# Local attention: two triangular probability blocks added, transposed and split as one, then separated by two GpSimd selections

## The chip, the core and the metric

The kernel runs on one core of a Trainium2 chip. A core has a matrix engine (TensorE, PE in the profile), three engines for element-wise work (VectorE or DVE, ScalarE or ACT, GpSimd or POOL), a queue that issues transfers (SyncE or SP), a scratch memory of 128 partitions (SBUF) and an accumulator memory (PSUM). Each engine works through its own instructions in order; semaphores make one engine wait for another. The metric is the device time of one execution in microseconds.

## The reference, cut to what matters

A decoder block with two parallel mixers over 1024 tokens, and a feed-forward part behind them. The change concerns the first mixer, local attention with a window of 128 keys: eight query heads in two groups of four, each group with one key/value head of width 64.

```
qb = q.reshape(B, nb, BLOCK, SWA_KV_HEADS, SWA_GROUP, HEAD_DIM)       # 8 blocks of 128 queries
...
diff = qi - kj + BLOCK                     # kj over 256 keys: the block before, and its own
band_ok = (diff >= 0) & (diff < WINDOW)
...
s = jnp.where(mask[None, :, None, None], s, -jnp.inf)
...
p = jnp.exp(s - m)
denom = jnp.sum(p, axis=-1, keepdims=True) + jnp.exp(sink - m)
p = (p / denom).astype(v.dtype)
o = jnp.einsum('bnhgqk,bnkhd->bnqhgd', p, vw)
```

For query `q` of a block, the allowed keys of the block before are those with index `k > q`, and those of its own block are `k <= q`. The probability block 128 x 256 of a head is therefore an upper and a lower triangle that complement each other, and all else in it is zero. The first block has no block before it.

## The kernel before, in words

All matrix products are made at nearly full float32 accuracy out of rounded parts: an operand is split into a high part (rounded copy, by ACT) and a low part (source minus high part, by DVE); the helper is `split` (L161 to L166). `mm3` (L168 to L174) issues three matmuls for a product: high by high, high by low, low by high.

Local attention runs in sixteen iterations, `it` = 0 to 15: group `it // 8`, query block `it % 8`. Iterations 0 and 8 are first blocks and have one key block, all others two. The iterations are threaded with `gate_step()` (L843), which issues one step of another, larger product (the gate projections): twelve matmuls of 128x512 with their weights split three steps ahead by ACT and DVE, and sums of weight tiles ("mixes", L177 and L180, 128x256 pieces) on POOL. The loop is L1018 to L1035. In iteration `it` it issues, in this order: a load of queries (`sw_q`), a gate step, the query transposes of `it+1` (`sw_qT`), a gate step, the value product of `it-1` (`sw_pv`), the scores and softmax of `it+1` (`sw_scores`), a gate step, and the probability transposes of `it` (`sw_pT`).

- `sw_scores` (L898 to L933): eight matmuls give the scores of four heads. DVE adds the band mask and takes the maximum (L914), ACT takes the exponentials with their sums (L926), and POOL adds the sink's term (L928), inverts the denominators (L929) and multiplies the probabilities `pe` (128 x 4 x 256) by them, a head at a time (L931).
- `sw_pT` (L935 to L944): for each key block, TensorE transposes the four heads' 128x128 blocks into one PSUM tile (L943), and `split` writes its high and low parts to `pth` and `ptl`.
- `sw_pv` (L946 to L965): for each key block two matmuls (L954 on `pth`, L955 on `ptl`) with the values as weights, then a copy on ACT (L957) and two additions on DVE (L962, L963).

TensorE and SP take their instructions in the order in which the program writes them (`in_order`, L328). In this loop ACT, DVE and POOL are ordered by a planner at build time, by its own costs; on the chip each of them is then in order too.

Of the kernel before, what the change touches and what calls it, by code (L numbers as in the profile page):

```python
# [9 lines left out]
F32R = mybir.dt.float32r  # L10
BF16 = mybir.dt.bfloat16
AF = mybir.ActivationFunctionType
ALU = mybir.AluOpType
# [4 lines left out]
P = 128  # L18
# [71 lines left out]
def hybrid_block_kernel(  # L90
# [29 lines left out]
    nc = tc.nc  # L120
# [19 lines left out]
    def uid(name):  # L140
        counter[0] += 1
        return f"{name}_{counter[0]}"

    def U(name, dt=F32, shape=(P, 1024)):
        return pool.tile(list(shape), dt, tag="u", name=uid(name))
# [4 lines left out]
    def tiny(name, w=1):  # L150
        return small.tile([P, w], F32, tag=f"t{w}", name=uid(name))

    def P1(name, shape=(P, 512)):
        return ps1.tile(list(shape), F32, tag="ps", name=uid(name))

    def PX(name, shape=(P, 512)):
        return psum["x"].tile(list(shape), F32, tag="ps", name=uid(name))
# [3 lines left out]
    def split(hi, lo, src, eng=None):  # L161

        i = nc.scalar.copy(hi, src)  # L163
        if held[0]:
            tc.keep_in_program_order(i)
        (eng or nc.vector).tensor_tensor(lo, src, hi.bitcast(F32), op=ALU.subtract)  # L166
# [15 lines left out]
    def blk(b, n=1):  # L182
        return slice(b * P, (b + n) * P)
# [5 lines left out]
    ident = const.tile([P, P], F32, name="ident")  # L189
# [708 lines left out]
    def sw_scores(it):  # L898
        g, b = divmod(it, NB)
        d = sw[it]  # L900
        qs = d.pop("qs")
        c0 = P if b == 0 else 0
        kc = slice((b - 1) * P + c0, (b + 1) * P)
        mx = tiny("mx", 4)
        scs = []
        for hp in range(2):
            sc = PX("sc", (P, 2, 2 * P))
            scs.append(sc)
            for j in range(2):
                nc.tensor.matmul(sc[:, j, c0:], qs[:, hp, j], khd[g][0][:, kc], start=True, stop=False)  # L910
                nc.tensor.matmul(sc[:, j, c0:], qs[:, hp, j], khd[g][1][:, kc], start=False, stop=True)
            for j in range(2):
                h = 2 * hp + j
                nc.vector.tensor_tensor_reduce(sc[:, j, c0:], sc[:, j, c0:], band[:, c0:], 1.0, NEG, op0=ALU.add,  # L914
                                               op1=ALU.max, accum_out=mx[:, h:h + 1])
        ns = nsink[:, 4 * g:4 * g + 4]
        nm = tiny("nm", 4)
        nc.vector.scalar_tensor_tensor(nm, mx, -SC_A, ns, op0=ALU.mult, op1=ALU.min)
        es = tiny("es", 4)
        nc.vector.tensor_tensor(es, nm, ns, op=ALU.subtract)  # L920
        den = tiny("den", 4)
        pe = U("pe", F32, (P, 4, 2 * P))
        for h in range(4):
            if h == 1:
                nc.scalar.activation(es, es, AF.Exp)
            nc.scalar.activation(pe[:, h, c0:], scs[h // 2][:, h % 2, c0:], AF.Exp, scale=SC_A, bias=nm[:, h:h + 1],  # L926
                                 accum_out=den[:, h:h + 1])
        nc.gpsimd.tensor_tensor(den, den, es, op=ALU.add)  # L928
        nc.gpsimd.tensor_tensor(den, den, neg_one, op=ALU.pow)  # L929
        for h in range(4):  # L930
            nc.gpsimd.tensor_scalar(pe[:, h, c0:], pe[:, h, c0:], den[:, h:h + 1], 0.0, op0=ALU.mult, op1=ALU.add)  # L931
        d["pe"] = pe
        d["kbs"] = [1] if b == 0 else [0, 1]  # L933

    def sw_pT(it):  # L935
        d = sw[it]
        pe = d.pop("pe")
        d["pth"] = U("pth", F32R, (P, 2, 4, P))
        d["ptl"] = U("ptl", F32R, (P, 2, 4, P))
        for kb in d["kbs"]:  # L940
            pp = P1("pT", (P, 4, P))
            for h in range(4):
                nc.tensor.transpose(pp[:, h], pe[:, h, blk(kb)], ident)  # L943
            split(d["pth"][:, kb], d["ptl"][:, kb], pp)  # L944

    def sw_pv(it):  # L946
        g, b = divmod(it, NB)
        d = sw.pop(it)
        kbs = d["kbs"]
        po = P1("o", (P, 2, 2, P))  # L950
        for kb in kbs:
            kblk = b - 1 + kb
            vst = vv[kblk // 4][:, kblk % 4, g]
            nc.tensor.matmul(po, vst, d["pth"][:, kb], start=kb == kbs[0], stop=False)  # L954
            nc.tensor.matmul(po, vst, d["ptl"][:, kb], start=False, stop=kb == 1)  # L955
        tmp = U("ot", F32, (P, 2, 2, P))
        nc.scalar.copy(tmp[0:64], po[64:128])  # L957
        if b % 4 == 0:
            oa_t[it // 4] = U("oa", F32, (P, 2, 512))
        oa = oa_t[it // 4]  # L960
        oc = blk(b % 4)
        nc.vector.tensor_tensor(oa[0:64, :, oc], po[0:64, :, 0], tmp[0:64, :, 0], op=ALU.add)  # L962
        nc.vector.tensor_tensor(oa[64:128, :, oc], po[0:64, :, 1], tmp[0:64, :, 1], op=ALU.add)  # L963
        if b % 4 == 3:
            nc.sync.dma_start(oa_d[it // 4], oa_t.pop(it // 4))  # L965
# [6 lines left out]
    for i, b in enumerate((4, 5, 6, 7, 0, 1, 2, 3)):  # L972
        ps = P1("kl", (P, KVL))
        mm3(ps, [(hT(k, blk(b)), (wkl[k // 4][0][:, k % 4], wkl[k // 4][1][:, k % 4])) for k in range(NK)])
        t = U("lat", F32, (P, 2, KVL))
        nc.scalar.copy(t[:, 0], ps)
        ss = tiny("ss")
        nc.scalar.activation(t[:, 1], t[:, 0], AF.Square, accum_out=ss)
        r = rstd_of(ss, KVL)
        if i == 0:  # L980
            latent_end(NB - 1)
            sw_qT(0)
            while lat_out:
                lat_store()
        if i == 2:
            gates.prep_to(1)
        if i == 3:
            gates.mix(0, nc.vector)
        if i == 4:
            sw_scores(0)  # L990
            gates.prep_to(2)
        if i >= 4:
            t4_of_h(i - 4)
        scaled.append((t, r, b))
        if i == 4:
            gates.load_part(1, 0)
        while len(scaled) > (2 if i < 5 else 1):
            kv_out(*scaled.pop(0))
# [19 lines left out]
    for it in range(N_SW):  # L1018
        if it + 2 < N_SW:
            sw_q(it + 2)  # L1020
        gate_step()
        if it + 1 < N_SW:
            sw_qT(it + 1)
        gate_step()
        if it >= 1:
            sw_pv(it - 1)
        if it + 1 < N_SW:
            sw_scores(it + 1)
        if it == N_SW - 1:
            load_lat(4)  # L1030
        gate_step()
        sw_pT(it)
    gate_step()
    gate_step()
    sw_pv(N_SW - 1)  # L1035
    in_order.__exit__(None, None, None)

# [233 lines left out]
    for t in range(NT):  # L1271
        h, n = divmod(t, NB)
# [509 lines left out]
```

## Time and profile before

| | |
|---|---|
| median of 3 runs | 1357.79 us (1356.15 to 1358.18) |
| span of the profiled execution | 1357.9 us |
| PE busy | 1338.8 us, 99% |
| DVE busy | 914.3 us, 67% |
| ACT busy | 641.1 us, 47% |
| POOL busy | 557.1 us, 41% |

The profile gives no other time for its execution than the span. Engines run beside each other, so busy shares add up to more than one. The local-attention loop lies between about 151 and 329 us.

In a row of the timeline stand the start and the length in us, the engine, the line, the operation, what it writes and reads, its shape and its count; in brackets, how long the engine had stood idle and what ended that. In a row of groups stand the count, the sum in us and the mean in ns, then the idle time before them.

### The profile page before, as it was taken

The page shows a single profiled execution, that of the slowest core. Times are in us where ns is not written, and L with a number is a line of the kernel's source. Part 1 is how long each engine was busy: PE and PEld are TensorE (multiplying, and loading weights), DVE is VectorE, ACT ScalarE, POOL GpSimd, SP SyncE. Part 2 cuts the span into 40 slices and gives each one's busy share as a digit, 9 for nine tenths or more (in the row PEclk, how much of TensorE's full clock was granted, in tenths as well). Part 3 has the DMA queues.
Part 4 walks back from the last instruction along what each step waited for, and adds up shares of the span by engine and source line. Part 5 has one row for each costly group of instructions (what it writes and reads, how often), then busy time and mean ns, then how long its engine had stood idle before and what let it go on. Part 6 is the DMA issues. An engine that isn't in the chain of part 4 may idle for free.

```text
span 1357.9 us, 18990 instructions
## 1 busy us (share of the span) xinstructions
PE 1338.8 (99%) x6600; PEld 1122.6 (83%) x6600; DVE 914.3 (67%) x1495; ACT 641.1 (47%) x1299; POOL 557.1 (41%) x610
## 2 busy tenths in 40 slices
PE   9999999999999999999999999999999999999997
PEld 6899878878888888888887888888888888888886
DVE  6868767776777787585448866666656654664862
ACT  7433767665567777651336232322332332644443
POOL 1115545553166554200031465766665551022521
PEclk9999999999999999999999999999999999999999
DMA  9454322335100110671243353644434425996504
GB/s 359 162 182 157 115 102 83 101 129 179 54 1 13 44 47 17 250 239 55 112 167 134 127 175 143 228 178 178 151 137 178 164 85 180 380 380 245 171 11 145
DMA packets 78239, 202.25 MB, mean 149 GB/s; under 512 B 8768, under 2 KB 15424, under 8 KB 78144
## 3 DMA queue, kind: packets, MB, share of 16 engines
q1 hardware_dynamic: 76704, 198.68, 41.2%
q10 hardware_dynamic: 1440, 2.36, 0.5%
q8 instruction: 52, 0.85, 0.2%
q14 instruction: 43, 0.35, 0.1%
HBM read 141.24 MB, written 59.77 MB: 148 GB/s over the span
## 4 chain that ended last, share of the span: by engine, by line
PE 79%; DVE 8%; ACT 4%; issue 3%; POOL 3%; DMA 2%; SPq 0%; POOLq 0%; ACTq 0%; DVEq 0%
PE fa L174 7%; PE fa L172 7%; PE fa L173 7%; PE fb L174 6%; PE fb L173 6%; PE fb L172 6%; PE fd L172 5%; PE fd L174 5%; PE fd L173 5%; PE xo L172 2%; PE xo L174 2%; PE xo L173 2%; PE pTb L1170 1%; PE oA L172 1%; PE oA L174 1%
## 5 line engine op out<-in xcount | busy, mean ns | idle before, releaser
L166 DVE TENSOR_TENSOR wl<-wr,wl 128x512 fp32r<-128x512 f32 x150 | 153.6, 1048 | 72.3 <-ACT wl L163 71.9
L166 DVE TENSOR_TENSOR lrv<-lr,lrv 128x1024 fp32r<-128x1024 f32 x77 | 104.9, 1396 | 48.6 <-ACT lrv L163 44.5
L163 ACT CAST lrv<-lr 128x1024 fp32r<-128x1024 f32 x77 | 80.1, 1052 | 94.1 <-PE fd L174 55.6
L172 PE MATMUL fd<-lrv 128*128 128x512 f32 x308 | 119.8, 389 | 0.0
L173 PE MATMUL fd<-lrv 128*128 128x512 f32 x308 | 119.8, 389 | 0.0
L174 PE MATMUL fd<-lrv 128*128 128x512 f32 x308 | 119.8, 389 | 0.0
L177 POOL TENSOR_TENSOR wr<-wr,sm 128x512 f32<-128x512 f32 (+1 forms) x38 | 46.4, 1229 | 150.8 <-DVE wl L166 117.2
L163 ACT CAST wl<-wr 128x512 fp32r<-128x512 f32 x150 | 86.9, 623 | 2.1 <-DVE wr L828 1.9
L304 POOL TENSOR_SCALAR ms<-ss 128x1 f32<-128x1 f32 x32 | 8.7, 271 | 189.8 <-ACT xn L1546 111.5
L166 DVE TENSOR_TENSOR wl<-sm,wl 128x512 fp32r<-128x512 f32 x60 | 47.2, 812 | 46.0 <-ACT wl L163 45.9
L174 PEld LDWEIGHTS fd<-lrv 128*128 128x128 f32 x308 | 57.8, 188 | 12.1
L173 PEld LDWEIGHTS fd<-lrv 128*128 128x128 f32 x308 | 57.8, 188 | 12.1
L172 PEld LDWEIGHTS fd<-lrv 128*128 128x128 f32 x308 | 57.8, 188 | 11.8
L1155 POOL TENSOR_TENSOR denb<-denb,neg_one 128x1 f32<-128x1 f32 x64 | 38.0, 594 | 69.2 <-ACT p L1154 56.8
L1154 ACT ACTIVATE p<-scb,nmb 128x384 f32<-128x384 f32 (+3 forms) x64 | 47.6, 744 | 38.4 <-DVE nmb L1153 36.5
L166 DVE TENSOR_TENSOR ptl<-pTb,pth 128x512 fp32r<-128x512 f32 (+2 forms) x96 | 50.5, 550 | 14.0 <-ACT pth L163 13.4
L1153 DVE CUSTOM_DVE_ANT_0 scb<-scb,mask 128x384 f32<-128x384 f32 (+3 forms) x64 | 48.5, 758 | 13.1 <-PE scb L1145 12.5
L1438 ACT ACTIVATE act<-sm 128x512 f32<-128x512 f32 x11 | 7.0, 633 | 104.9 <-DVE sm L180 104.9
L1156 POOL TENSOR_SCALAR p<-p,denb 128x384 f32<-128x384 f32 (+3 forms) x64 | 49.4, 773 | 6.3
L163 ACT CAST pth<-pTb 128x512 fp32r<-128x512 f32 (+2 forms) x96 | 43.3, 482 | 12.2 <-PE pTb L1170 11.6
L172 PE MATMUL fb<-t2h,wl 128*128 128x512 f32 x120 | 47.4, 395 | 0.0
L172 PE MATMUL fb<-t3h,wl 128*128 128x512 f32 x120 | 47.3, 394 | 0.0
(348 smaller groups left out, 4310.2 us busy)
## 6 DMA issues: line engine op xcount, KB each, us to landing
lr<-la_d SPq DMA_DIRECT2D x77, 256.0 KB, 5.4
wr<-in_w_gate_dram SPq DMA_DIRECT2D x22, 512.0 KB, 3.9
wr<-in_w_up_dram SPq DMA_DIRECT2D x22, 512.0 KB, 5.1
wd<-in_w_down_dram SPq DMA_DIRECT2D x22, 512.0 KB, 6.6
rb_d<-wd SPq DMA_DIRECT2D x22, 512.0 KB, 2.6
la_d<-sd SPq DMA_DIRECT2D x22, 512.0 KB, 5.3
lr<-rb_d SPq DMA_DIRECT2D x44, 256.0 KB, 5.4
lr<-in_w_down_dram SPq DMA_DIRECT2D x33, 256.0 KB, 5.8
```

The lines of the kernel that those rows point to most:

```text
L163: i = nc.scalar.copy(hi, src)
L166: (eng or nc.vector).tensor_tensor(lo, src, hi.bitcast(F32), op=ALU.subtract)
L172: nc.tensor.matmul(ps, ah, bh, start=first and i == 0, stop=False, skip_group_check=go_on)
L173: nc.tensor.matmul(ps, ah, bl, start=False, stop=False, skip_group_check=go_on)
L174: nc.tensor.matmul(ps, al, bh, start=False, stop=last and i == n - 1, skip_group_check=go_on)
L177: eng.tensor_tensor(out, a, b, op=ALU.subtract)
L304: nc.gpsimd.tensor_scalar(ms, ss, 1.0 / width, EPS, op0=ALU.mult, op1=ALU.add)
L1153: nc.vector.tensor_tensor_reduce(s_, s_, m_, 1.0, -NEG, op0=ALU.add, op1=ALU.min, accum_out=nm)
L1154: nc.scalar.activation(p_, s_, AF.Exp, scale=-1.0, bias=nm, accum_out=den)
L1155: nc.gpsimd.tensor_tensor(den, den, neg_one[:, 0:1], op=ALU.pow)
L1156: nc.gpsimd.tensor_scalar(p[:, 0:w], p[:, 0:w], den, 0.0, op0=ALU.mult, op1=ALU.add)
L1170: nc.tensor.transpose(pp[:, i], p[:, blk(k0 + i)], ident)
```

## The change

For every iteration with two key blocks, POOL now adds the two halves of `pe` before the multiplication, which then covers 128 columns a head and not 256. `sw_pT` transposes four blocks and not eight, and splits once, into one tile `x` that holds the high and the low part (128 x 2 x 4 x 128). Two affine selections on POOL then separate the triangles: one writes a second tile `y` with the entries `q >= k` of the own block and zeros elsewhere, the other clears these in `x`, in place, so that `x` keeps the block before. `sw_pv` issues the same four matmuls on slices of `x` and `y`. First blocks (iterations 0 and 8) have one half, one transposition of four blocks and no selection.

```diff
+        if b:
+            nc.gpsimd.tensor_tensor(pe[:, :, 0:P], pe[:, :, 0:P], pe[:, :, P:2 * P], op=ALU.add)
+        cp = slice(0, P) if b else slice(P, 2 * P)
         for h in range(4):
-            nc.gpsimd.tensor_scalar(pe[:, h, c0:], pe[:, h, c0:], den[:, h:h + 1], 0.0, op0=ALU.mult, op1=ALU.add)
+            nc.gpsimd.tensor_scalar(pe[:, h, cp], pe[:, h, cp], den[:, h:h + 1], 0.0, op0=ALU.mult, op1=ALU.add)
...
-        d["pth"] = U("pth", F32R, (P, 2, 4, P))
-        d["ptl"] = U("ptl", F32R, (P, 2, 4, P))
-        for kb in d["kbs"]:
-            pp = P1("pT", (P, 4, P))
-            for h in range(4):
-                nc.tensor.transpose(pp[:, h], pe[:, h, blk(kb)], ident)
-            split(d["pth"][:, kb], d["ptl"][:, kb], pp)
+        pp = P1("pT", (P, 4, P))
+        for h in range(4):
+            nc.tensor.transpose(pp[:, h], pe[:, h, blk(d["kbs"][0])], ident)
+        x = U("pt", F32R, (P, 2, 4, P))
+        split(x[:, 0], x[:, 1], pp)
+        if len(d["kbs"]) == 2:
+            y = U("pt", F32R, (P, 2, 4, P))
+            nc.gpsimd.affine_select(y, x, [[0, 8], [1, P]], ALU.is_ge, 0.0, base=0, channel_multiplier=-1)
+            nc.gpsimd.affine_select(x, x, [[0, 8], [-1, P]], ALU.is_ge, 0.0, base=-1, channel_multiplier=1)
+            d["pt"] = [x, y]
+        else:
+            d["pt"] = [None, x]
...
-            nc.tensor.matmul(po, vst, d["pth"][:, kb], start=kb == kbs[0], stop=False)
-            nc.tensor.matmul(po, vst, d["ptl"][:, kb], start=False, stop=kb == 1)
+            nc.tensor.matmul(po, vst, d["pt"][kb][:, 0], start=kb == kbs[0], stop=False)
+            nc.tensor.matmul(po, vst, d["pt"][kb][:, 1], start=False, stop=kb == 1)
```

In the changed program the addition is L931, the multiplication L934, the transposes L943 as before, the selections L948 (into `y`) and L949 (in place), and the matmuls of `sw_pv` L962 and L963.

## The prediction

> **What bounds the kernel now.** I read the page from the top: busy shares, then the chain that ended last, then the stage that the diff touches.
>
> ```profile
> span 1357.9 us, 18990 instructions
> PE 1338.8 (99%) x6600; PEld 1122.6 (83%) x6600; DVE 914.3 (67%) x1495; ACT 641.1 (47%) x1299; POOL 557.1 (41%) x610
> ...
> PE 79%; DVE 8%; ACT 4%; issue 3%; POOL 3%; DMA 2%; SPq 0%; POOLq 0%; ACTq 0%; DVEq 0%
> ```
>
> TensorE is busy 99% of the span, so a TensorE instruction that is removed is worth its whole time as long as nothing else becomes late, and a new TensorE wait costs its whole length. The span, 1357.9 us, stands beside a median of 1357.79 us over the runs, so sums against the span may be read against the median.
>
> The diff touches the sixteen local-attention iterations. The view by stages, cut from the first matmul of the first `sw_pv` to that of the last (one number per engine, busy us; clock and DMA behind):
>
> ```profile
> 157.49:327.68 170.19, 167.20 (x852) 139.56 (x851) 125.37 (x306) 110.20 (x302) 92.06 (x141) 1.00 0.32 107
> ```
>
> Here too PE is the bound: 167.2 of 170.2 us. POOL is busy 92.1 us, 54%. On that average the stage has room for more POOL work. The average doesn't decide, though: PE takes its instructions in the written order, so the question is when POOL has a result that PE stands waiting for. The timeline of PE gives the beat of an iteration (start, length, then the instruction; L954 is the first matmul of `sw_pv`, L943 the probability transposes):
>
> ```profile
> 157.49 0.39 PE L954 MATMUL o<-pth,vv 128*128 128x512 f32 x1
> ...
> 168.42 0.39 PE L954 MATMUL o<-pth,vv 128*128 128x512 f32 x1
> 168.87 0.39 PE L954 MATMUL o<-pth,vv 128*128 128x512 f32 x1
> ...
> 170.28 0.40 PE L172 MATMUL fb<-t2h,wl 128*128 128x512 f32 x1
> ...
> 173.03 1.03 PE L943 MATMUL pT<-ident,pe 128*128 128x128 f32 x8
> ...
> 179.64 0.39 PE L954 MATMUL o<-pth,vv 128*128 128x512 f32 x1
> ...
> 238.15 0.39 PE L954 MATMUL o<-pth,vv 128*128 128x512 f32 x1
> 242.76 0.60 PE L943 MATMUL pT<-ident,pe 128*128 128x128 f32 x4
> 248.92 0.39 PE L954 MATMUL o<-pth,vv 128*128 128x512 f32 x1
> ...
> 317.69 0.39 PE L954 MATMUL o<-pth,vv 128*128 128x512 f32 x1
> ...
> 327.68 0.39 PE L954 MATMUL o<-pth,vv 128*128 128x512 f32 x1
> ```
>
> One iteration takes 11.22 us (168.42 to 179.64). And the timeline of POOL, which normalizes the probabilities of the next iteration:
>
> ```profile
> 174.89 0.20 POOL L928 TENSOR_TENSOR den<-den,es 128x4 f32<-128x4 f32 x1 [3.69 <-ACT pe L926]
> 175.17 1.02 POOL L929 TENSOR_TENSOR den<-den,neg_one 128x4 f32<-128x4 f32 x1
> 176.29 2.35 POOL L931 TENSOR_SCALAR pe<-pe,den 128x256 f32<-128x256 f32 x4
> ...
> 193.10 0.74 POOL L177 TENSOR_TENSOR wr<-wr 128x256 f32<-128x256 f32 x1
> ...
> 254.95 0.20 POOL L928 TENSOR_TENSOR den<-den,es 128x4 f32<-128x4 f32 x1 [4.17 <-ACT pe L926]
> ```
>
> The first multiplications end at 178.64. The transposes that need them run about 11 us after those at 173.03, at some 184.2, so POOL has over 5 us of slack today.
>
> **The change, part by part.** *Transposes.* Fourteen iterations (all but the first block of each group) lose four of eight. Eight extend over 1.03 us and four over 0.60, and the eight start 0.13 us apart (272 ns is the length of one); four fewer are 4 x 0.13 = 0.51 us. This is on the path: 14 x 0.51 = 7.2 us to gain. PE's own beat becomes 11.22 - 0.51 = 10.7 us.
>
> *Splits.* Half of these go:
>
> ```profile
> L163 ACT CAST pth<-pT x30: 585/614/627, 154.7 to 322.4; 128x512 fp32r<-128x512 f32 x30
> L166 DVE TENSOR_TENSOR ptl<-pT,pth x30: 674/682/693, 155.3 to 323.3; 128x512 fp32r<-128x512 f32 x30
> ```
>
> 14 x 0.61 us of ACT and 14 x 0.68 us of DVE lie beside PE's gate matmuls; I cost this at nothing. Without that cover it would be a gain of at most 1.3 us an iteration.
>
> *POOL.* Each of the fourteen gains an addition of 128x4x128 and two selections of 128x1024, and its four multiplications shrink from 128x256 to 128x128. The rows by form, mean ns last but one:
>
> ```profile
> L931 POOL TENSOR_SCALAR pe<-pe,den 128x256 f32<-128x256 f32 x56 | 31.6, 581 | 1.2
> L1156 POOL TENSOR_SCALAR p<-p,denb 128x1024 f32<-128x1024 f32 x8 | 9.0, 1125 | 0.8
> L1156 POOL TENSOR_SCALAR p<-p,denb 128x128 f32<-128x128 f32 x8 | 3.0, 373 | 0.8
> masks.py:199 POOL TENSOR_SCALAR_AFFINE_SELECT ident<-ident 128x128 f32<-128x128 f32 x1 | 0.3, 292 | 0.1
> L177 POOL TENSOR_TENSOR sd<-act,sd 128x512 f32<-128x512 f32 x11 | 14.3, 1298 | 0.2
> L177 POOL TENSOR_TENSOR wr<-wr 128x512 f32<-128x512 f32 x20 | 33.0, 1648 | 0.0
> ```
>
> The multiplications become 4 x 0.373 = 1.5 us. The addition has the size of the 128x512 rows, 1.30 to 1.65 us; I take 1.35. A selection of this size isn't in the trace. The 128x128 one took 0.292 us. Growing from there like the multiplication, (1125 - 373) / 896 = 0.84 ns an element, gives 292 + 896 x 0.84 = 1.04 us; eight of them, 8 x 0.292 = 2.34 us, is the other end. I take 1.2, near the one-input row of the same size (1.125). Both selections and their gaps are then 2.5 us.
>
> A rule of the Trainium skill points higher: GPSIMD Engine Reference, section 7, says that a compare-then-select body on GpSimd costs 2.03 cycles per element, 1.03 when unrolled. With its 1.2 GHz that is an estimate of 1.73 us for 1024 elements, and the sum below would end 14 us higher, near 1409. The 292 ns row, fixed part included, fits either slope, so no run here shows which holds.
>
> *Who waits.* The selections stand in the in-order POOL queue. In the changed program's instruction order they come behind the next iteration's normalization, and the first matmul of `sw_pv` waits for both (the second writes in place):
>
> ```
> POOL L928 TensorTensor den_2071<-den_2071,es_2069 128x4 [waits Activation]
> POOL L931 TensorTensor pe_2072<-pe_2072 128x4x128
> POOL L929 TensorTensor den_2071<-den_2071,neg_one 128x4
> POOL L934 TensorScalarPtr pe_2072<-pe_2072,den_2071 128x128 x4
> POOL L948 TensorScalarAffineSelect pt_2114<-pt_2111 128x1024 [waits DVE]
> POOL L949 TensorScalarAffineSelect pt_2111<-pt_2111 128x1024 [waits Pool]
> PE   L962 Matmult o_2167<-pt_2111,vv_156 128x512 [waits Activation,Pool]
> ```
>
> So `sw_pv(it)` waits for the exponentials of `it+1`. These follow the scores that PE issues right behind `sw_pv(it-1)`. That closes a ring: `sw_pv(it-1)` to the start of L928, 168.42 to 174.89 = 6.47 us; L928 to L929 0.28; addition and gap 1.4; L929 to the multiplications 1.12; these 1.5 and a gap 0.1; selections 2.5; the signal to PE 0.1, by the gap between L928's end and L929 (0.08). Together 6.47 + 7.0 = 13.5 us against PE's 10.7. PE stands 2.8 us in each such iteration, and the stall stays in the ring: every engine behind it is shifted too. Behind the waiting matmul are the scores of the iteration after next and all later gate matmuls.
>
> Thirteen iterations have this ring: `it` 1 to 7 and 9 to 14. Iterations 0 and 8 have no selection, 15 has no normalization ahead of it, and iteration 7 saves the addition (block 8 is narrow).
>
> *Gate mixes.* In six of the thirteen the changed order has pieces of the gate sums ahead of the last selection: 5, 2 and 1 of them, twice. They cost
>
> ```profile
> L177 POOL TENSOR_TENSOR sm<-sm,wr 128x256 f32<-128x256 f32 x14 | 11.6, 827 | 0.2
> L180 POOL TENSOR_TENSOR sm<-wr,wr 128x256 f32<-128x256 f32 x14 | 11.0, 796 | 2.0 <-ACT wr L830 2.0
> ```
>
> 16 x 0.8 = 12.8 us, today hidden in POOL's idle time, then on the ring.
>
> *Sum.* From the first `sw_pv` to the last: 13 x 13.5 - 1.4 + 12.8 = 186.9; the step 7 to 8 stays PE's, 248.92 - 238.15 = 10.77; the last, 327.68 - 317.69 = 9.99, loses 0.51. Together 207.1 us instead of 170.2: 37 us more, 1395 us. DMA issues don't change in number, and SP's order differs nowhere that matters; POOL and SP queues behind the loop are only shifted.
>
> *Bounds.* Low: selection 1.04, addition 1.30, ring start 254.95 - 248.92 = 6.03 us (the shortest that I find for a full block; DVE and ACT fall less behind when PE waits), mixes 16 x 0.74: a ring of 12.7 and 26 us more, 1383. High: selection 2.34, addition 1.65: a ring of 16.1, 70 us more, 1428.
>
> **Rivals.** *Faster: the selections are on time.* PE would keep only the removed transposes: 1357.9 - 7.2 = 1350.7 us. It needs POOL to be done within PE's 10.7 us. Ring start and normalization alone are 6.47 + 4.4 = 10.9, so this holds only if selections run ahead of the multiplications. For it speaks a row of DVE:
>
> ```profile
> 175.96 1.28 DVE L166 TENSOR_TENSOR ptl<-pT,pth 128x512 fp32r<-128x512 f32 x2
> ```
>
> The first of today's two split remainders ends near 176.6, so the selections' input is there before the multiplications end. Against it: the queue's order.
>
> *Slow selections:* 1409 to 1428 us, by the upper price. POOL would be busy 9.3 us of 16, so the ring, not its occupancy, would still set the time.
>
> *PE's clock falls in the stalls.* The profile shows 1.00 throughout, but also
>
> ```profile
> 1.23 3.59 PE L503 MATMUL warm<-warm 128*128 128x512 bf16 x8 [1.23 <-DVE warm L500]
> ...
> 201.00 0.50 PE L172 MATMUL fa<-hh,wl 128*128 128x512 f32 x1 [1.51 <-ACT pu L805]
> ```
>
> the first eight matmuls at 0.45 us apiece, where two of `sw_pv` take 0.45 together (168.42 to 168.87): PE does run at half speed after idling. An idle 1.51 us cost only one longer matmul. The stalls would be 2.8 us, and 3.6, 4.4 and 6.8 with mixes. If the six long ones slow the `sw_pv` and scores behind them (1.86 us, from 168.42 to the gate matmul at 170.28) by as much again, that is 6 x 1.86 = 11 us, 1406. The Trainium skill, TensorE: Matmul & The Clock Gate, section "HAM oscillation", has such a rule: gaps of PE over about 3.4 us bring the half clock back.
>
> *Softer:* DVE and ACT catch up more than in the low bound, or mixes wait elsewhere: 10 to 20 us more, 1368 to 1378.
>
> **How the numbers follow.** The ring with my prices 0.64; slow selections 0.14; clock 0.10; softer 0.07; selections on time 0.05. Forecast 1395. The range 1380 to 1425 leaves out the faster and softer cases and the very end of the slow one, under 2 in 10. About 0.2% (2.7 us) is what a measurement here can tell from no change. Faster 0.04, same 0.01, slower 0.95.
>
> **What would show it.** Right: L943 in groups of four; `sw_pv` 13 to 14 us apart; PE idle before L962 put down to POOL L949, in sum 35 to 45 us; POOL's L928 idle less. Wrong: L949 ending before the gate matmuls ahead of `sw_pv` do, a selection under 0.8 us or over 2.4, or the granted clock below 1.00 in the loop.

## The result, and the profile after

The changed kernel takes 1409.27 us (median of 4 runs, 1405.79 to 1411.2) against 1357.8 us before: a ratio of 1.0377, 95% interval 1.0365 to 1.0389, slower by 51.5 us. The profiled execution has a span of 1409.5 us.

From the page of the changed kernel, the busy shares and the chain that ended last:

```profile
span 1409.5 us, 18897 instructions
PE 1352.3 (96%) x6544; PEld 1127.7 (80%) x6544; DVE 919.5 (65%) x1481; ACT 634.8 (45%) x1285; POOL 604.7 (43%) x652
...
PE 68%; POOL 10%; DVE 10%; ACT 5%; issue 4%; DMA 2%; SPq 0%; POOLq 0%; ACTq 0%; DVEq 0%
```

56 matmuls fewer, and PE is nevertheless busy for 13.5 us more. POOL's share of the chain rose from 3% to 10%. The same stage as in the prediction, from the first matmul of the first `sw_pv` to that of the last, and below it pieces of it that begin with a `sw_pv` (length, then busy us of PE, PEld, DVE, ACT and POOL, then the granted clock):

```profile
158.22:378.69 220.47, 180.53 (x795) 145.25 (x794) 131.32 (x291) 103.45 (x287) 136.48 (x181) 0.91 0.25 82
...
187.32:192.06 4.74, 4.74 (x24) 4.02 (x25) 2.82 (x12) 0.82 (x2) 0.65 (x1) 1.00 0.00 0
204.79:212.21 7.42, 7.42 (x24) 6.19 (x25) 2.82 (x12) 2.25 (x9) 0.00 (x0) 0.60 0.35 89
...
237.68:243.97 6.29, 6.29 (x24) 5.35 (x25) 2.82 (x12) 1.34 (x5) 3.44 (x5) 0.73 0.47 139
```

The stage grew from 170.19 to 220.47 us, by 50.3: nearly the whole loss lies here. It splits in two. PE is idle for 220.47 - 180.53 = 39.9 us where it was idle for 3.0; that is 36.9. And it is busy for 180.53 us instead of 167.20, 13.3 more, though some 6 us of transposes are gone: PE takes some 19 us longer over the work that is left. The granted clock says why: 1.00 after some waits, 0.60 or 0.73 over a whole run of value product, scores and gate step after others.

What ended PE's waits in the loop, from the view of waits (sum, times, longest), and three `sw_pv` with their waits from the timeline:

```profile
PE o L962 <- POOL pt L949: 39.0, 13, 6.3
```

```profile
172.63 0.49 PE L962 MATMUL o<-pt,vv 128*128 128x512 f32 x1 [2.81 <-POOL pt L949]
...
187.32 0.50 PE L962 MATMUL o<-pt,vv 128*128 128x512 f32 x1 [2.10 <-POOL pt L949]
...
204.79 0.79 PE L962 MATMUL o<-pt,vv 128*128 128x512 f32 x1 [6.25 <-POOL pt L949]
```

Thirteen waits, all on the second selection. POOL between two of these `sw_pv`:

```profile
180.09 0.20 POOL L928 TENSOR_TENSOR den<-den,es 128x4 f32<-128x4 f32 x1 [6.12 <-ACT pe L926]
180.24 1.28 POOL L931 TENSOR_TENSOR pe<-pe 128x512 f32<-128x512 f32 x1
181.48 1.47 POOL L929 TENSOR_TENSOR den<-den,neg_one 128x4 f32<-128x4 f32 x1
183.05 1.50 POOL L934 TENSOR_SCALAR pe<-pe,den 128x128 f32<-128x128 f32 x4
184.51 1.60 POOL L948 TENSOR_SCALAR_AFFINE_SELECT pt<-pt 128x1024 fp32r<-128x1024 f32 x1
186.18 1.09 POOL L949 TENSOR_SCALAR_AFFINE_SELECT pt<-pt 128x1024 fp32r<-128x1024 f32 x1
```

This is the ring: value product at 172.63, L928 at 180.09, L949 done at 187.27, next value product at 187.32. POOL had stood idle for 6.1 us before L928. The selections' input, the low part that DVE writes, was there while POOL was at the inversion:

```profile
182.00 0.68 DVE L166 TENSOR_TENSOR pt<-pT,pt 128x512 fp32r<-128x512 f32 x1
```

It was ready at 182.68, and the first selection began at 184.51: it waited for its turn in the queue for 1.8 us, where PE's whole wait was 2.10. The groups of the loop give the prices that the trace of before could not show:

```profile
L931 POOL TENSOR_TENSOR pe<-pe 128x512 f32<-128x512 f32 x14 | 18.1, 1292 | 0.0
L949 POOL TENSOR_SCALAR_AFFINE_SELECT pt<-pt 128x1024 fp32r<-128x1024 f32 x14 | 16.9, 1210 | 0.8
L948 POOL TENSOR_SCALAR_AFFINE_SELECT pt<-pt 128x1024 fp32r<-128x1024 f32 x14 | 16.7, 1193 | 4.0 <-DVE pt L166 4.0
```

### The profile page after: what moved, and what is told of

Its sections match the earlier page's. It is cut to its first block, busy times and chain, and to the rows that moved or that the text cites. A ratio compares the mean times of both kernels' runs of the same rounds, so it can differ in the third digit from the quotient of the medians.

```text
span 1409.5 us, 18897 instructions
## 1 busy us (share of the span) xinstructions
PE 1352.3 (96%) x6544; PEld 1127.7 (80%) x6544; DVE 919.5 (65%) x1481; ACT 634.8 (45%) x1285; POOL 604.7 (43%) x652
## 4 chain that ended last, share of the span: by engine, by line
PE 68%; POOL 10%; DVE 10%; ACT 5%; issue 4%; DMA 2%; SPq 0%; POOLq 0%; ACTq 0%; DVEq 0%
PE fa L174 6%; PE fa L172 6%; PE fa L173 6%; PE fd L173 5%; PE fd L172 5%; PE fd L174 5%; PE fb L172 4%; PE fb L173 4%; PE fb L174 4%; PE xo L174 2%; PE xo L173 2%; PE xo L172 2%; POOL pe L934 2%; ACT pe L926 2%; PE pTb L1178 1%
## 5 line engine op out<-in xcount | busy, mean ns | idle before, releaser
L172 PE MATMUL fd<-lrv 128*128 128x512 f32 x308 | 119.8, 389 | 0.0
L166 DVE TENSOR_TENSOR wl<-sm,wl 128x512 fp32r<-128x512 f32 x60 | 54.5, 935 | 45.4 <-ACT wl L163 45.3
L172 PEld LDWEIGHTS fd<-lrv 128*128 128x128 f32 x308 | 57.8, 188 | 12.1
L1162 ACT ACTIVATE p<-scb,nmb 128x384 f32<-128x384 f32 (+3 forms) x64 | 47.6, 744 | 38.4 <-DVE nmb L1161 36.9
L1161 DVE CUSTOM_DVE_ANT_0 scb<-scb,mask 128x384 f32<-128x384 f32 (+3 forms) x64 | 48.5, 758 | 13.3 <-PE scb L1153 12.7
L962 PE MATMUL o<-pt,vv 128*128 128x512 f32 x30 | 16.0, 533 | 39.0 <-POOL pt L949 39.0
L914 DVE CUSTOM_DVE_ANT_0 sc<-sc,band 128x256 f32<-128x256 f32 (+1 forms) x64 | 26.0, 413 | 37.4 <-PE sc L911 36.6
```

The costliest lines, as they stand in the source:

```text
L172: nc.tensor.matmul(ps, ah, bh, start=first and i == 0, stop=False, skip_group_check=go_on)
L1161: nc.vector.tensor_tensor_reduce(s_, s_, m_, 1.0, -NEG, op0=ALU.add, op1=ALU.min, accum_out=nm)
L1162: nc.scalar.activation(p_, s_, AF.Exp, scale=-1.0, bias=nm, accum_out=den)
```

## The experiments

Two theories at the start. Theory: PE loses the time in the ring, because the selections stand in POOL's queue behind the next iteration's normalization. Rival: POOL has too much work in all, whatever its order. A second question was why the result exceeds the forecast by 14 us: PE's clock after its waits, or something in the ring itself. Ratios are to the kernel before, run on the same chip.

### e1: the value product one iteration later

```diff
-        if it >= 1:
-            sw_pv(it - 1)
+        if it >= 2:
+            sw_pv(it - 2)
...
+    sw_pv(N_SW - 2)
     gate_step()
     gate_step()
     sw_pv(N_SW - 1)
```

> The value product of an iteration is issued one iteration later, so that its selections have a whole beat more; nothing else of the change is touched. Theory (the stall is the ring sw_pv - scores - exponentials - normalization - selections - sw_pv): the ring is open, PE waits on no selection, the granted clock is 1.00 in the loop, and only the 7.2 us of removed transposes are left: 1351 us, up to 1362 if POOL, which then has some 9.7 us of work in a beat of 10.7, makes other waits. Rival (POOL simply has too much work, or its selections slow DVE by sharing its memory): giving the selections more time doesn't help, 1390 us or more.

1368.5 us, ratio 1.0076 (1.0059 to 1.0093). PE's wait for the selections is gone, and with it 41 us, though POOL's work is what it was. This is what the theory of the ring says, and far from the rival's 1390. But the time is 6 us above the expected range, and the granted clock is 0.96 from the first `sw_pv` to the last, not 1.00. PE's own waits in the loop are now these:

```profile
PE fa L172 <- ACT pu L805: 7.4, 2, 3.7
PE fb L174 <- DVE wl L166: 2.4, 3, 0.8
PE fa L174 <- DVE wl L166: 1.2, 2, 0.6
```

The first is the pair of waits that was 1.5 and 1.2 us before the change:

```profile
PE fa L172 <- ACT pu L805: 2.7, 2, 1.5
```

ACT makes PE wait because it stands itself in front of the split of a gate sum that POOL has late. From e1 again:

```profile
192.90 0.62 ACT L163 CAST wl<-sm 128x512 fp32r<-128x512 f32 x1 [5.24 <-POOL sm L177]
```

### e2: the removed transposes issued again

```diff
-        for h in range(4):
-            nc.tensor.transpose(pp[:, h], pe[:, h, blk(d["kbs"][0])], ident)
+        for kb in d["kbs"]:
+            for h in range(4):
+                nc.tensor.transpose(pp[:, h], pe[:, h, blk(d["kbs"][0])], ident)
```

> The four removed transposes are issued again (the same four blocks twice), 14 x 0.51 us of PE work. Theory: they fall into PE's wait for the selections, so what the change takes from PE is worth nothing here: within 3 us of the changed kernel's 1409. Rival (PE's work still counts beside the stalls): 7 us more, 1416.

1406.6 us, ratio 1.0362 (1.0346 to 1.0377): 2.7 us under the changed kernel, within the spread of both, and not 7 us over it (nor 6, which is nearer to what the transposes cost; see the part on the prediction). As theory has it, the saved PE work is worth nothing while PE waits in the same iteration. But the wait took up only 2.8 us of the added work: it is 36.2 us instead of 39.0. The clock of the stage was also higher, 0.93 instead of 0.91; whether the fuller PE or chance did that isn't shown.

### e3: one selection left out

```diff
-            nc.gpsimd.affine_select(x, x, [[0, 8], [-1, P]], ALU.is_ge, 0.0, base=-1, channel_multiplier=1)
```

> The second selection (in place, 1.2 us each) is left out, so the tile of the block before keeps both triangles and the output is not the reference's. Theory: each of the thirteen rings is 1.25 us shorter, 16 us less, 1393, and up to 8 us less still where the shorter stall no longer brings the half clock: 1385 to 1394. Rival (the stall is set by the normalization or by ACT, the selection only ends last): no more than 5 us less, 1404 or more.

1379.1 us, ratio 1.0158 (1.0143 to 1.0173): 30 us less, more than the 15 to 24 expected. The direction and the rival's end are clear. What the expectation missed: without the in-place selection the first two of the four matmuls need no selection at all, so the wait also moves two matmuls back, some 0.6 us a ring, and PE's waits in all fall to 19.3 us, ten of them of 0.9 to 1.4 us and two of 4.3. With them the clock of the stage rises from 0.91 to 0.96, and PE is busy for some 11 us less over the same matmuls.

### e4: the waits filled with idle matmuls

```diff
+        fill = {1: 9, 2: 6, 3: 22, 4: 9, 5: 6, 6: 6, 9: 8, 10: 18, 11: 13, 12: 10, 13: 2, 14: 11}
+        for _ in range(fill.get(it, 0)):
+            nc.tensor.matmul(po, vv[0][:, 0, g], khd[g][0][:, 0:512], start=True, stop=True)
         for kb in kbs:
```

> Idle matmuls (2 to 22 of 128x512 per iteration, some 0.23 us each, into the tile that the value product then overwrites) are put ahead of the waiting matmul, sized to about three quarters of the wait that the profile shows there. They add no work to the ring. Theory (the 14 us by which the result exceeds the predicted 1395 come for the larger part from PE running at a lower granted clock after its waits): the granted clock stays at 1.00, the ring start falls from about 7.1 to 6.5 us, 1397 to 1402 us in spite of 114 matmuls more. Rival (the ring is longer for another reason, as DVE and ACT in another order): 1409 or more.

1402.2 us, ratio 1.0326 (1.0311 to 1.0342): 7 us less with 120 matmuls more (the table's sum; the expectation says 114). The same place as above, the value product of iteration 3, in the timeline of PE, with the start of L928 behind it on POOL, and the clock of the piece between:

```profile
201.75 0.50 PE L965 MATMUL o<-pt,vv 128*128 128x512 f32 x1 [1.33 <-POOL pt L949]
```

```profile
208.36 0.20 POOL L928 TENSOR_TENSOR den<-den,es 128x4 f32<-128x4 f32 x1 [6.67 <-ACT pe L926]
```

```profile
201.75:206.50 4.75, 4.75 (x25) 4.03 (x26) 2.83 (x12) 0.83 (x2) 0.00 (x0) 1.00 0.24 91
```

The clock is 1.00 where it was 0.60, and the start of the ring takes 208.36 - 201.75 = 6.61 us. In the changed kernel it took 7.9 at this place. Over the whole stage the clock is 0.98 instead of 0.91. So the slow clock behind the waits is a cause of the excess, and half of the 14 us went with it.

### e5: only POOL's order changed

```diff
-        nc.gpsimd.tensor_tensor(den, den, neg_one, op=ALU.pow)
...
+    def sw_norm(it):
...
+    pool_by_hand = tc.manual_schedule(engines={engines.Pool})
+    pool_by_hand.__enter__()
     for it in range(N_SW):
...
         sw_pT(it)
+        if it + 1 < N_SW:
+            sw_norm(it + 1)
+    pool_by_hand.__exit__(None, None, None)
```

`sw_norm` holds the inversion and the four multiplications.

> The changed kernel's instructions, none added or taken away; only POOL's order in the loop is written by hand: after the sink term and the addition of iteration it+1 come the selections of it, and only then the inversion and the multiplications of it+1 (the gate sums stand where the program writes them). Theory (the order in POOL's queue makes the stall): the selections wait for the split at 8.2 us after sw_pv and end at 10.8, about PE's beat of 10.7, so most of the stall goes; what stays are the iterations where gate sums of 1.4 to 4.5 us stand ahead of the selections, some 14 us in sum: 1360 to 1375. Rival (the amount of work on POOL, whatever its order): 1400 or more.

1379.5 us, ratio 1.0156 (1.0141 to 1.0171). The same instructions in another order on one engine give 30 us back. The rival, the amount of work, falls. The time is 4.5 us above the expected range: PE still waits 17.4 us for the selections, in eleven waits, the two longest, 3.9 and 4.0 us, where six pieces of a gate sum stand ahead of them. The bare ring has no slack left either: its waits are 0.5 to 0.7 us without gate sums.

### e6, e7, e8: work moved to DVE

All three begin from e1. e6 replaces the second selection by a subtraction, e7 moves the addition, e8 does both.

```diff
-            nc.gpsimd.affine_select(x, x, [[0, 8], [-1, P]], ALU.is_ge, 0.0, base=-1, channel_multiplier=1)
+            nc.vector.tensor_tensor(x, x.bitcast(F32), y.bitcast(F32), op=ALU.subtract)
...
-            nc.gpsimd.tensor_tensor(pe[:, :, 0:P], pe[:, :, 0:P], pe[:, :, P:2 * P], op=ALU.add)
+            nc.vector.tensor_tensor(pe[:, :, 0:P], pe[:, :, 0:P], pe[:, :, P:2 * P], op=ALU.add)
```

> e1 (value product one iteration later) with the second selection replaced by x - y on DVE. What stayed in e1, PE waiting 7.4 us for ACT behind late gate sums on POOL, is put down by theory to POOL being nearly full (9.7 of 10.7 us in a beat). Theory: POOL loses 1.2 us a beat and the gate sums come in time, 1352 to 1362. Rival (the gate sums are late by their place in the order, not by load): no more than 3 us less than e1, 1365 or more.

> e1 with the addition of the two halves on DVE instead of POOL (1.3 us a beat less on POOL, ahead of the normalization and of the gate sums). Theory of load, and that of place too, since all behind the addition moves ahead: 1352 to 1362. If DVE delays it (its queue holds the gate splits): 1365 or more.

> e1 with the subtraction and the addition both on DVE; POOL is left with one selection and has some 7.2 us of work in a beat, less than with the kernel before plus a selection. Theory: no wait on POOL remains and the 7.2 us of transposes show: 1350 to 1356, faster than the kernel before. Rival (DVE, which gets 2.1 us a beat and loses 0.7, becomes late): 1360 or more.

e6: 1405.5 us, 1.0351 (1.0335 to 1.0366). e7: 1358.3 us, 1.0002 (0.999 to 1.0014). e8: 1393.0 us, 1.0257 (1.024 to 1.0274). Both with the subtraction are far worse than e1, for a reason that neither theory had; that the times lie above the rivals' bounds doesn't show those rivals. The timeline of DVE in e6:

```profile
182.50 1.23 DVE L949 TENSOR_TENSOR pt<-pt,pt 128x1024 fp32r<-128x1024 f32 x1 [2.37 <-POOL pt L948]
183.76 0.42 DVE L894 TENSOR_TENSOR qs<-qT,qs 64x256 fp32r<-64x256 f32 x1
184.21 0.43 DVE L895 TENSOR_TENSOR qs<-qT,qs 64x256 fp32r<-64x256 f32 x1
```

```profile
PE sc L910 <- DVE qs L894: 30.1, 11, 5.6
```

DVE is in order too. The subtraction waits there for the selection, which still stands behind the normalization on POOL, and behind the subtraction stand the query splits that PE's next scores need. It is the old ring again, closed through another engine: 30.1 us of waits. e7, which has nothing on DVE that waits for a selection, takes 10 us off e1.

### e9 to e12: the gate sums moved or ordered

e9 is the kernel before with the gate sums on DVE, e10 is e1 with that, e11 is e7 with that; e12 is e7 with POOL's loop order as the program writes it.

```diff
+            eng = eng or self.mix_eng
             for m in self.ms:
```

`mix_eng` is `nc.vector` (DVE) for the gates.

> The kernel before with the gate sums (three of 128x512 per gate tile) on DVE instead of POOL; nothing of the change. A control for the next two. The kernel before has two PE waits of 1.5 and 1.2 us on ACT, itself behind late gate sums. Theory: these go, 2 to 3 us less, 1355; if DVE's in-order queue makes the sums late in its turn, 1358 or more.

> e1 (value product one iteration later) with the gate sums on DVE; the addition and both selections stay on POOL. Theory of POOL's load: the 7.4 us that PE waits for ACT behind late gate sums in e1, and the slower clock behind them, go: 1350 to 1358. If the addition on POOL keeps the normalization late, 1360 or more.

> e7 (value product one iteration later, addition on DVE) with the gate sums on DVE too. Theory: no PE wait is left in the loop and the removed transposes show in full, 7.2 us under the kernel before plus its own two waits of 2.7: 1348 to 1352. Rival (DVE, with some 1.6 us a beat more, becomes late): 1356 or more.

> e7 with POOL's order in the loop as the program writes it: the gate sums stand whole behind a normalization, not one piece ahead of it and the rest among it. Theory: the sums come at about the time they do in e7, so PE's wait of 6.1 us for ACT stays within 2 us and the time within 4 us of e7's 1358. Rival (the planner's order costs this wait): 1354 or less.

| | us | ratio, 95% interval |
|---|---|---|
| e9 | 1357.7 | 0.9997 (0.9989 to 1.0006) |
| e10 | 1363.5 | 1.004 (1.0027 to 1.0053) |
| e11 | 1356.0 | 0.9979 (0.9971 to 0.9988) |
| e12 | 1364.1 | 1.0038 (1.0023 to 1.0053) |

e11 beats the kernel before, by 0.2%, or 2.9 us by the ratio; e9 shows that moving the gate sums alone doesn't, though PE's two waits for ACT in front of L172 shrink there from 2.7 us to one of 0.8. In e11 no wait of PE in the loop is over 0.7 us. Yet it was expected at 1348 to 1352. A part of that was never to be had: the transposes cost some 6 us and not 7.2. The beats of e11 from transposes to transposes are 10.4 to 12.0 us, the last one 9.6; where the rest goes is open.

e10 differs from e11 only in where the addition runs, and is 7.5 us slower, outside its main expectation and inside the other, but only by its number: it isn't the normalization that is late. PE waits 5.5 us for low parts that DVE delivers late (the last section says why). e12 missed its bound by 2 us: PE's wait for ACT is 7.4 us instead of e7's 6.1 and short waits for DVE came back, so the planner's order wasn't what cost e7 that wait. That rival falls.

## Why the prediction was right, point by point

- **The ring and its place.** Right. Thirteen waits, in the named iterations, 39.0 us in sum, put down to L949; e1 and e5 open the ring by time and by order alone, and the time follows.
- **The removed transposes.** Right that four instead of eight run, and that nothing is gained from it while PE waits (e2). The price was too high: transposes start 0.11 us apart and not 0.13, and the prediction's own lines, 1.03 us for eight and 0.60 for four, give 0.43 us an iteration, 6.0 in all and not 7.2.
- **Selections at 1.2 us.** 1.19 and 1.21 us in the mean. The shortest rows take 1.09, so the low end of 1.04 was near for the bare instruction. The eight longer rows, 1.43 to 1.60, all ran beside a gate split on DVE. The estimate of 1.73 us from the Trainium skill's GPSIMD Engine Reference, section 7 (2.03 cycles per element for compare and select), was too high here; 1.09 us is nearer to that section's unrolled 1.03 cycles, an estimate of 0.88 us at the same 1.2 GHz, without fixed costs. The sum by that rule, 1409, met the time by chance.
- **The addition at 1.35 us.** 1.29.
- **From L928 to the value product, 7.0 us.** About 7.2 without gate sums (180.09 to 187.32 = 7.23). The inversion behind the addition took 1.57 us up to the multiplications (181.48 to 183.05), where the prediction had 1.12.
- **The gate sums on the ring.** Right in kind. Seventeen pieces and not sixteen, one more in iteration 14.
- **The sum, 37 us.** Short by 14. The first matmul of the last `sw_pv` moved from 327.68 to 378.69 us, by 51.0. Term by term: the thirteen starts of the ring took 92.4 us and not 13 x 6.5 = 84.5, 7.9 more; POOL's part with the gate sums took 105.5 and not 13 x 7.0 - 1.4 + 12.8 = 102.4, 3.1 more; the two steps left to PE took 2.2 more, 1.8 of it in the last, where the clock fell too; the first value product came 0.7 later. Together 13.9.
- **The step that was mis-sized** is the start of the ring, taken as 6.47 us from a place in the trace of before where PE doesn't wait. The seven slow ones of the changed kernel took 7.2 to 7.9, the six others 6.5 in the mean, as forecast. The difference is PE's clock, which the prediction had as a rival with a chance of 0.10 and 11 us. Ring and clock were not alternatives: the one brings the other. The prediction let only the six longest waits slow PE, from 3.6 us on, and for 1.86 us each; in the trace the clock fell after 2.2 to 2.8 us too, and by stretches of 3.41 us (last section).
- **Its own signs.** L943 in groups of four, the waits put down to L949 and their sum came as named. The granted clock in the loop was 0.91, and a clock below 1.00 stood among the signs of being wrong: it is the one that came. Two signs of being right didn't: the value products of the rings were 11.3 to 18.0 us apart, 15.2 in the mean, and not 13 to 14; and POOL idled more before L928, not less.

The groups of L928 on POOL and of L914 on DVE in the loop, before:

```profile
L928 POOL TENSOR_TENSOR den<-den,es 128x4 f32<-128x4 f32 x15 | 3.0, 201 | 72.3 <-ACT pe L926 72.3
...
L914 DVE CUSTOM_DVE_ANT_0 sc<-sc,band 128x256 f32<-128x256 f32 x54 | 23.0, 427 | 3.9 <-PE sc L911 3.4
```

and after:

```profile
L928 POOL TENSOR_TENSOR den<-den,es 128x4 f32<-128x4 f32 x15 | 3.0, 202 | 80.9 <-ACT pe L926 80.9
...
L914 DVE CUSTOM_DVE_ANT_0 sc<-sc,band 128x256 f32<-128x256 f32 x54 | 23.0, 428 | 37.2 <-PE sc L911 36.6
```

So the prediction had the mechanism and most of the loss. But the case that came is its rival of the falling clock, 1406 us with a chance of 0.10, and not the one behind its 1395. That this rival's 11 us lie near the measured excess of 14 is in part luck, as it counted fewer and shorter slow pieces than there were.

The selections were late in all thirteen rings, and no softer case came. DVE and ACT did catch up: before L914, the first step behind the scores, DVE stood idle for 3.9 us in the loop before the change and for 37.2 after it, nearly all of it until the scores came. But what follows the scores on DVE and ACT takes its time even so, and the six starts that the clock didn't lengthen came out at 5.9 to 7.0 us.

## What to carry to other kernels

Before an in-order engine gets work whose result the bound engine waits for, follow what stands ahead of it in that queue: here a share of 54% said there was room, and the queue's order made a ring that no spare time could fill. Giving the consumer one more iteration was worth 41 us (e1), and giving the producer another place in its queue 30 us (e5), as much as leaving out one of the two selections (e3); and moving the dependent work to another in-order engine can close the same ring there. Price a stall of TensorE above its length, since the work behind it may run at a lower clock.

## What the runs showed of the hardware that I had not expected

**The clock fell after short waits.** 0.73 over the 6 us behind a wait of 2.23 us (at 237.68), 0.60 behind 6.25 us, but 1.00 behind 2.10 (at 187.32). The Trainium skill, TensorE: Matmul & The Clock Gate, section "HAM oscillation", puts the gap at about 3.4 us; the traces agree that a gap lowers the clock, and show it from shorter ones. In the changed kernel's trace the granted clock is half for nine stretches of 3.41 or 6.83 us in the loop, 41 us in all, and full between them. Cut into steps of 3.41 us from the edges of these stretches, the trace shows when (length, then PE's busy time first, then the clock behind the five engines):

```profile
183.36:186.77 3.41, 1.87 (x9) 1.20 (x7) 2.23 (x4) 2.39 (x6) 3.34 (x6) 1.00 0.33 111
186.77:190.19 3.42, 2.87 (x16) 2.56 (x17) 1.15 (x5) 0.58 (x1) 1.20 (x2) 1.00 0.02 7
...
197.01:200.43 3.42, 1.53 (x7) 0.94 (x5) 1.90 (x4) 0.00 (x0) 3.42 (x7) 1.00 0.20 77
200.43:203.84 3.41, 0.00 (x0) 0.00 (x0) 1.61 (x2) 0.62 (x1) 3.26 (x5) 1.00 0.00 0
203.84:207.25 3.41, 2.46 (x7) 2.07 (x8) 0.67 (x1) 0.35 (x1) 0.90 (x1) 0.50 0.00 0
...
336.96:340.37 3.41, 1.50 (x8) 1.32 (x9) 0.93 (x2) 0.26 (x1) 3.41 (x5) 1.00 0.43 125
340.37:343.78 3.41, 3.41 (x13) 2.83 (x11) 2.82 (x12) 0.70 (x3) 1.96 (x3) 0.50 0.28 106
```

In this loop a step at full clock with PE idle for 1.91 us or more (the least is 3.41 - 1.50 = 1.91) was followed by half clock each time, and one with 1.89 us or less (the most is 3.42 - 1.53 = 1.89) never. The wait of 2.10 us lay across an edge, with 1.54 us before it and 0.55 behind, and brought nothing. So it is not the length of a wait alone that counts, but how much of it falls into one step. In the other runs the border is less sharp: there, idle times of 1.70 to 1.91 us came with either.

**A POOL addition doubles a DVE split beside it.** From the changed kernel, DVE's gate split of 128x512 and the addition that ran on POOL at that time, and a split of the same size on DVE later:

```profile
154.24 1.52 DVE L166 TENSOR_TENSOR wl<-sm,wl 128x512 fp32r<-128x512 f32 x1 [3.04 <-ACT wl L163]
...
156.29 0.68 DVE L166 TENSOR_TENSOR wl<-wr,wl 128x512 fp32r<-128x512 f32 x1
```

```profile
153.93 1.29 POOL L931 TENSOR_TENSOR pe<-pe 128x512 f32<-128x512 f32 x1
```

1.52 us instead of 0.68, and PE waited 0.76 us for it; the forecast had put the addition's whole cost on POOL. In the loop all fourteen gate splits that lay mostly beside this addition took 1.47 to 1.54 us, and those with POOL idle 0.68 or 0.69; the mean of all gate splits rose from 0.79 to 1.09. With the addition on DVE (e11 against e10) the waits of this kind are gone, 7.5 us. The Trainium skill's GPSIMD Engine Reference, section 8, says that the two engines share their way into the scratch memory, with contention where a DVE instruction has two inputs from there, as this split has; this agrees. The addition isn't the only one: nine gate splits beside a first selection, with one input, took 0.69 to 1.59 us. The seven beside the small inversion (128x4) took 0.68.
